# Prompt attention with undivided probabilities: low halves on GpSimd, weights' low halves on VectorE

## The chip, the cores and the metric

One NeuronCore of a Trainium2 chip runs the program. The metric is the time of one execution on the device in microseconds (us); of the kernel before, three runs are known. Times within a run are counted from the start of the profiled span.

## What is computed

The reference is one layer of a decoder step with 1024 prompt tokens and 8 sample tokens, model width 1024, all in float32. A normed input is projected (`w_in`); a third of the mixing width is attention, the rest a pooling mixer and a spatial-gating MLP; each is multiplied by a SiLU gate and all go through one output projection (`w_out`), a second norm and the residual. For the attention of the prompt (8 heads of 64, 2 key/value heads, an ALiBi slope per head) three branches are added, each with its own softmax and a sigmoid gate per token and head:

```python
s = jnp.where(mask, s, NEG_INF)
p = jnp.exp(s - jnp.max(s, axis=-1, keepdims=True)) * mask
return p / jnp.maximum(jnp.sum(p, axis=-1, keepdims=True), 1e-30)
...
o = gf[..., 0:1] * o_c + gf[..., 1:2] * o_s + gf[..., 2:3] * o_w
```

`o_c` attends to 16 compressed blocks, `o_s` to selected blocks (with 16 blocks in all these are all keys up to the token), `o_w` to a window of 512 keys.

## The kernel before

Float32 accuracy is kept on the matmul engine by splitting every operand into a high and a low float16 half; a product is then three matmuls (high by high, high by low, low by high). Weights are loaded in float32 by SyncE (`load_w`) or, for the output weights, by GpSimd (`load_wo`), ScalarE writes the high half (64 times the weight, line 254 or 1452) and the low half is made by VectorE in one operation (lines 260 and 1457) or by GpSimd in two (lines 257 and 258, 1454 and 1455). In the part that matters here, GpSimd makes them for six projection tiles (`if "attn" in hold`) and for every second output tile (`q % 2`).

The first 250 us project keys, values and queries and serve the sample tokens. Then `AT` is opened and the prompt's attention runs, from token tile 7 down to 0 (128 tokens each). Its work is cut into units (token tile, first head, number of heads): one head for tiles 7 to 3, two for tiles 2 and 1, four for tile 0, fifty units in all. Tile i has `i + 1` key tiles in the selected branch and `min(i + 1, 5)` in the window branch. The loop over `st` is a pipeline written out by hand. In step `st` it does:

* `norm_a` of the unit before: VectorE makes the factor gate / sum (lines 1328 and 1329), ScalarE writes the high half H of the divided probabilities, one copy per head and branch (line 1334);
* `qk` of the unit: scores on TensorE into the banks `s`; per branch VectorE adds slope and mask, keeps the row's minimum in `sm` (line 1320), and ScalarE takes the exponential and its sum (line 1322) into P, which has two buffers;
* `norm_b` of the unit before: VectorE writes the low half of the divided probabilities, one operation per head and branch (line 1343), and SyncE issues one transposing DMA from H (two buffers) to T (three buffers, line 1346);
* `take`: a budget of other work, that is the remaining projections (`tgroup`), pooling, gating and output projections (`outproj`); most chunks fill one of the two `fp` banks and are evicted by VectorE or ScalarE at the next `flush`;
* `pv` of the unit three steps back: per head and key tile one matmul of 128 columns (high T by high and low V) and one of 64 (low T by high V), both branches into the same columns; at the end of a half of the heads the compressed part is added with three matmuls of 256 columns;
* `combine` when half of the heads are done (line 1383 ff.): ScalarE and VectorE add the two column blocks, multiply by the gate, and write both halves for the output projection.

SyncE and GpSimd run in the written order; for the other engines the framework chooses an order that respects the dependencies. Waiting times for GpSimd are written down with `later(...)`, by which generators such as `post_u` and `gmlp` decide when their next part is emitted.

Of the kernel before, what the change touches and what calls it, by code (L numbers as in the profile page):

```python
# [20 lines left out]
EPS = 1e-6  # L21
SLOTS = [(k, g) for g in range(4) for k in range(2)]
# [28 lines left out]
def tile_hymba(ctx: ExitStack, tc: tile.TileContext, A: dict):  # L51
# [17 lines left out]
    # ------------------------------------------------------------ emission order  # L69
# [81 lines left out]
    # ------------------------------------------------------------ tiles  # L151
# [22 lines left out]
    rsc = C.tile([128, 8], F32, name="rsc")  # L174
    md = C.tile([128, 2, 4, 8], F16, name="md")
# [49 lines left out]
    # ------------------------------------------------------------ loads and splits  # L225
# [19 lines left out]
    def split_w(gi):  # L245
# [108 lines left out]
    # ------------------------------------------------------------ start: two column groups, contraction outermost  # L354
# [112 lines left out]
    def bcast():  # L467
        for q in range(2):
# [3 lines left out]
            def done(q=q, pr=pr):  # L472
                S.activation(R[:, q * 512:q * 512 + 512], pr, AF.Copy)
                if q == 1:
# [3 lines left out]
                    V.tensor_scalar(rsc, rst, 2.0 ** -17, None, ALU.mult)  # L478
                    V.tensor_scalar(psc2, ccd("psc"), 1.0 / 128, None, ALU.mult)
# [40 lines left out]
    # ------------------------------------------------------------ column groups, features on partitions  # L520
# [38 lines left out]
    # ------------------------------------------------------------ compressed keys and values  # L559
# [104 lines left out]
    # ------------------------------------------------------------ compressed attention of the prompt  # L664
# [47 lines left out]
    # ------------------------------------------------------------ decode attention  # L712
# [170 lines left out]
    # ------------------------------------------------------------ column groups, tokens on partitions  # L883
# [157 lines left out]
    # ------------------------------------------------------------ pooling and gating  # L1041
# [160 lines left out]
    # ------------------------------------------------------------ projections that attention needs, decode beside them  # L1202
# [51 lines left out]
    # ------------------------------------------------------------ prompt attention, the rest of the projections between  # L1254
# [4 lines left out]
    # kl and the high parts of q once more, on the other half of the partitions: two low passes run side by side  # L1259
# [16 lines left out]

    def qk(u):
# [3 lines left out]
        sm = AT.tile([128, nh, 4], F32, tag="sm", name=f"sm{i}_{s0}", bufs=4)  # L1281
        if s0 % 4 == 0 and (i, s0) != (0, 4):
            load_qx(*((i, 1) if s0 == 0 else (i - 1, 0)))
        for h in range(nh):
# [31 lines left out]
            for (br, n, o), (ps, z) in zip(spans(i), banks):  # L1316
# [4 lines left out]
                                       sm[:, h, br:br + 1])  # L1321
                S.activation(p, p, AF.Exp, bias=sm[:, h, br:br + 1], scale=-1.0, accum_out=sm[:, h, 2 + br:3 + br])  # L1322
        return P, sm

    def norm_a(u, P, sm):
        i, s0, nh = u
        nt = i + 1 + min(i + 1, 5)
        V.scalar_tensor_tensor(sm[:, :, 2:4], sm[:, :, 2:4], 1e-30, invg[:, i, s0:s0 + nh, 1:3], ALU.max, ALU.mult)  # L1328
        V.reciprocal(sm[:, :, 2:4], sm[:, :, 2:4])
        H = AT.tile([128, 2, nh, nt * 128], F16, tag="H", name=f"H{i}_{s0}", bufs=2)  # L1330
        for h in range(nh):
            for br, n, o in spans(i):
                c = slice(o * 128, (o + n) * 128)
                S.activation(H[:, 0, h, c], P[:, h, c], AF.Copy, scale=sm[:, h, 2 + br:3 + br])  # L1334
        return H

    def norm_b(u, P, sm, H):
        i, s0, nh = u
        nt = i + 1 + min(i + 1, 5)
        for h in range(nh):  # L1340
            for br, n, o in spans(i):
                c = slice(o * 128, (o + n) * 128)
# [6 lines left out]
    obank = {}  # L1349

    def pv(u, pt):
        i, s0, nh = u
        nt = i + 1 + min(i + 1, 5)
        if s0 % 4 == 0:
            obank[i, s0 // 4] = op.tile([128, 512], F32, tag="o", name=f"O{i}_{s0 // 4}")
        ob = obank[i, s0 // 4]
        for h in range(nh):
            s = s0 + h
            c = slice(s % 2 * 64, s % 2 * 64 + 64)
            o = ob[:, s % 4 * 128:s % 4 * 128 + 128]  # L1360
            first = s % 4 == 0
            for br, n, off in spans(i):
                for j in range(n):
# [5 lines left out]
        if (s0 + nh) % 4 == 0:  # L1369
            need(f"pct{i // 4}")  # L1370
            pct = hold[f"pct{i // 4}"]
            b0 = i % 4
            oh = ob.rearrange("p (s h d) -> p s h d", h=2, d=64)[:, :, 0]
# [443 lines left out]
```

## Time and profile before

| What | Value |
|---|---|
| Runs | 608.74 us median of 3 (608.67 to 609.25) |
| Profiled execution, span | 610.4 us |
| TensorE busy | 540.0 us (88%) |
| VectorE busy | 470.7 us (77%) |
| ScalarE busy | 340.2 us (56%) |
| GpSimd busy | 200.4 us (33%) |

The profiled execution is 1.7 us above the median. In the rows further down PE is TensorE (PEld its weight loads), DVE VectorE, ACT ScalarE, POOL GpSimd and SP SyncE; "L1343" is line 1343 of the kernel. A busy share is a mean over stages that are limited by different engines, so it is read by stage.

### The profile page before, as it was taken

What the parts mean: (1) busy time and instruction counts of PE and PEld (TensorE: products, weight loads), DVE (VectorE), ACT (ScalarE), POOL (GpSimd) and SP (SyncE); (2) the same over time, 40 slices, a digit from 0 to 9 for tenths busy, and PEclk for the clock granted to TensorE, in tenths of its full rate; (3) what the DMA queues carried; (4) which work ended last, traced back from release to release, by engine and by line L of the source; (5) the groups of instructions that cost most, each with busy time, mean ns of one, the idle gap of its engine ahead of it and who ended that gap; (6) DMA issues with size and microseconds to landing.
All of it is one profiled execution on the core that took longest, in us unless ns stands there. A gap on an engine that the chain in (4) does not pass through costs nothing.

```text
span 610.4 us, 13331 instructions
## 1 busy us (share of the span) xinstructions
PE 540.0 (88%) x5188; PEld 348.1 (57%) x5188; DVE 470.7 (77%) x900; ACT 340.2 (56%) x662; POOL 200.4 (33%) x149
## 2 busy tenths in 40 slices
PE   5899989889999997999888997884659999999995
PEld 2566645579768997456555654453225454455552
DVE  5975489995784673598899999976997678887743
ACT  6444344464543452468665665655567667786831
POOL 1884395202345000354534347224643200000001
PEclk9989999998999999899998999887577899999999
DMA  8614884454735626179796949669798779879683
GB/s 294 241 35 134 232 219 116 116 157 120 230 125 178 214 71 187 42 123 188 115 159 119 176 76 177 120 136 181 176 178 177 133 102 208 177 135 220 138 196 120
DMA packets 196882, 95.24 MB, mean 156 GB/s; under 512 B 166867, under 2 KB 185715, under 8 KB 196755
## 3 DMA queue, kind: packets, MB, share of 16 engines
q1 hardware_dynamic: 194018, 81.37, 61.0%
q0 software_dynamic: 2656, 12.77, 6.2%
q8 instruction: 40, 0.66, 0.4%
q10 hardware_dynamic: 144, 0.26, 0.1%
q14 instruction: 24, 0.19, 0.1%
HBM read 45.43 MB, written 11.86 MB: 94 GB/s over the span
## 4 chain that ended last, share of the span: by engine, by line
PE 47%; DMA 19%; DVE 17%; SPq 6%; issue 6%; ACT 4%; POOL 2%; DVEq 0%; POOLq 0%; ACTq 0%
PE op L67 12%; PE ps L67 11%; DMA T<-H 10%; PE s L67 7%; PE zps L67 5%; DVE H L1343 5%; PE O L67 5%; DVE P L1320 2%; PE v1ps L67 2%; SPq L310 2%; DMA xm<-in_xT_dram 1%; ACT P L1322 1%; DMA raw<-in_wt_dram 1%; DVE qa L518 1%; SPq L317 1%
## 5 line engine op out<-in xcount | busy, mean ns | idle before, releaser
L67 PE MATMUL ps<-xh,ws 128*128 128x344 f16 x768 | 178.7, 316 | 6.7 <-DVE t L490 3.9
L67 PEld LDWEIGHTS <-ws 128*128 128x128 f16 x1376 | 129.1, 100 | 91.4 <-issue 19.5
L1322 ACT ACTIVATE P<-P,sm 128x640 f32<-128x640 f32 (+7 forms) x128 | 92.7, 725 | 62.9 <-DVE sm L1320 52.0
L67 PE MATMUL ps<-xl,ws 128*128 128x344 f16 x384 | 121.3, 316 | 0.0
L1343 DVE SCALAR_TENSOR_TENSOR H<-P,sm,H 128x640 f16<-128x640 f32 (+7 forms) x128 | 109.9, 899 | 10.2 <-ACT H L1334 10.1
L67 PEld LDWEIGHTS <-qa 128*128 128x128 f16 (+1 forms) x612 | 47.9, 98 | 87.6 <-issue 59.2
L1334 ACT ACTIVATE H<-P,sm 128x640 f16<-128x640 f32 (+7 forms) x128 | 84.9, 722 | 16.1 <-DMA T<-H 13.3
L1320 DVE CUSTOM_DVE_ANT_0 P<-s,ctt 128x640 f32<-128x640 f32 (+7 forms) x128 | 85.6, 701 | 10.4 <-PE s L67 10.0
L67 PE MATMUL O<-vn,T 128*128 128x128 f16 (+1 forms) x1056 | 59.4, 216 | 18.5 <-DMA T<-H 18.4
L67 PE MATMUL s<-ka,qa 128*128 128x384 f16 (+4 forms) x192 | 54.0, 338 | 20.5 <-DVE sm L1320 20.5
L67 PEld LDWEIGHTS <-T 128*128 128x128 f16 x1056 | 53.5, 103 | 28.9 <-DMA T<-H 22.5
L67 PEld LDWEIGHTS <-xh 128*128 128x128 f16 x768 | 61.3, 99 | 0.7
L67 PE MATMUL op<-wo,qa 128*128 128x512 f16 x192 | 46.6, 387 | 0.5 <-DMA qa<-yza 0.5
L67 PE MATMUL zps<-ws,xh 128*128 128x128 f16 x512 | 45.0, 219 | 0.0
L67 PE MATMUL zps<-ws,xl 128*128 128x128 f16 x256 | 43.6, 219 | 0.0
L257 POOL TENSOR_SCALAR raw<-raw 128x1024 f32<-128x1024 f32 x6 | 18.0, 3008 | 73.8 <-ACT ws L254 73.8
L1490 POOL TENSOR_SCALAR sq<-sq 128x1 f32<-128x1 f32 x8 | 2.1, 266 | 115.5 <-ACT o L1520 115.5
L67 PEld LDWEIGHTS <-xl 128*128 128x128 f16 x384 | 38.0, 99 | 2.7 <-issue 2.1
L254 ACT ACTIVATE ws<-raw 128x1024 f16<-128x1024 f32 x21 | 22.2, 1057 | 21.8 <-PE ps L67 11.0
L67 PE MATMUL s<-kl,qa 64*128 64x384 f16 (+5 forms) x100 | 33.7, 344 | 0.0
L67 PE MATMUL s<-klx,qx 64*128 64x384 f16 (+4 forms) x92 | 30.6, 333 | 0.0
L1328 DVE SCALAR_TENSOR_TENSOR sm<-sm,invg 128x2 f32<-128x2 f32 (+2 forms) x50 | 21.1, 422 | 8.0 <-ACT P L1322 7.8
(329 smaller groups left out, 931.6 us busy)
## 6 DMA issues: line engine op xcount, KB each, us to landing
raw<-in_wt_dram SPq DMA_DIRECT2D x21, 512.0 KB, 4.2
wor<-in_wo_dram POOLq DMA_DIRECT2D x8, 512.0 KB, 5.5
xr<-in_xn_dram SPq DMA_DIRECT2D x8, 512.0 KB, 4.4
o_kww_dram<-in_cwin_dram POOLq DMA_DIRECT2D x1, 4088.0 KB, 17.0
o_y_dram<-o SPq DMA_DIRECT2D x7, 512.0 KB, 4.2
cr<-in_ccmp_dram SPq DMA_DIRECT2D x24, 128.0 KB, 2.8
xq<-in_xT_dram SPq DMA_DIRECT2D x3, 516.0 KB, 8.5
kr<-in_cselk_dram SPq DMA_DIRECT2D x20, 64.0 KB, 2.0
```

The lines of the kernel that those rows point to most:

```text
L67: nc.tensor.matmul(out, lhsT=l, rhs=r, start=st, stop=en)
L254: S.activation(ws[:, 0, :, a:b], r, AF.Copy, scale=64.0)
L257: G.tensor_scalar(r, r, 64.0, None, ALU.mult)
L310: Y.dma_start(t[:, :, j * 128:(j + 1) * 128], A["ccmp"][page(b, j)].rearrange("o p (r c) -> (o p) r c", r=2))
L317: Y.dma_start(t[:, 0, j * 128:(j + 1) * 128], A["csel" + kv][page(b, j)].rearrange("o p c -> (o p) c"))
L518: V.tensor_tensor(qa[b:b + 64, :, 2 * g + k], tv[a:a + 64], qa[a:a + 64, :, 2 * g + k], ALU.subtract)
L1320: V.tensor_tensor_reduce(p, ps[:, z:z + T], ctt[:, end - T:end], -slope, 3e38, ALU.add, ALU.min, sm[:, h, br:br + 1])
L1322: S.activation(p, p, AF.Exp, bias=sm[:, h, br:br + 1], scale=-1.0, accum_out=sm[:, h, 2 + br:3 + br])
L1328: V.scalar_tensor_tensor(sm[:, :, 2:4], sm[:, :, 2:4], 1e-30, invg[:, i, s0:s0 + nh, 1:3], ALU.max, ALU.mult)
L1334: S.activation(H[:, 0, h, c], P[:, h, c], AF.Copy, scale=sm[:, h, 2 + br:3 + br])
L1343: V.scalar_tensor_tensor(H[:, 1, h, c], P[:, h, c], sm[:, h, 2 + br:3 + br], H[:, 0, h, c], ALU.mult, ALU.subtract)
L1490: G.tensor_scalar(sq[:, 2:3], sq[:, 1:2], 1.0 / 1024, sq[:, 0:1], ALU.mult, ALU.add)
```

## The change

In `qk`, both score passes of a head come first, then one addition of LN = ln 1024 to the head's two minima, then both exponentials. Right after, ScalarE writes the high half of the undivided probabilities, one copy for the whole unit. `norm_a` goes. `norm_b` becomes `low`: GpSimd subtracts H from P in one operation for the unit, then the transposing DMA is issued as before. `pv` keeps the branches apart, with three matmuls of 64 columns per key tile, and the compressed part moves to a bank and a tile of its own (`cmp_out`, once per token tile, ahead of the first unit's PV). `combine` divides: it makes the factors for four heads and two branches, multiplies, and adds the two branches and the compressed part. All weights' low halves go to VectorE. The sums of a token tile live in one tile (`sums`), and the memory for software DMA descriptors is set to 8192.

```diff
             S.activation(ws[:, 0, :, a:b], r, AF.Copy, scale=64.0)
-            if "attn" in hold:
-                later(3.8)
-                G.tensor_scalar(r, r, 64.0, None, ALU.mult)
-                G.tensor_tensor(ws[:, 1, :, a:b], r, ws[:, 0, :, a:b], ALU.subtract)
-            else:
+            if True:
                 V.scalar_tensor_tensor(ws[:, 1, :, a:b], r, 64.0, ws[:, 0, :, a:b], ALU.mult, ALU.subtract)
...
                 V.tensor_tensor_reduce(p, ps[:, z:z + T], ctt[:, end - T:end], -slope, 3e38, ALU.add, ALU.min,
-                                       sm[:, h, br:br + 1])
-                S.activation(p, p, AF.Exp, bias=sm[:, h, br:br + 1], scale=-1.0, accum_out=sm[:, h, 2 + br:3 + br])
+                                       sm[:, s, br:br + 1])
+            V.tensor_scalar(sm[:, s, 0:2], sm[:, s, 0:2], LN, None, ALU.add)
+            for br, n, o in spans(i):
+                p = P[:, h, o * 128:o * 128 + n * 128]
+                S.activation(p, p, AF.Exp, bias=sm[:, s, br:br + 1], scale=-1.0, accum_out=sm[:, s, 2 + br:3 + br])
+        H = AT.tile([128, 2, nh, nt * 128], F16, tag="H", name=f"H{i}_{s0}", bufs=2)
+        S.activation(H[:, 0], P, AF.Copy)
...
-                V.scalar_tensor_tensor(H[:, 1, h, c], P[:, h, c], sm[:, h, 2 + br:3 + br], H[:, 0, h, c],
-                                       ALU.mult, ALU.subtract)
+        G.tensor_tensor(H[:, 1], P, H[:, 0], ALU.subtract)
...
+    def cmp_out(i):
+        need(f"pct{i // 4}")
+        pct = hold[f"pct{i // 4}"]
+        b0 = i % 4
+        ps = fp.tile([128, 512], F32, tag="f", name=f"oc{i}")
+        for h in range(2):
+            c = slice(h * 256, h * 256 + 256)
+            mm(ps[:, c], pct[:, b0], vbd[:, 0, c], h == 0, False)
+            mm(ps[:, c], pct[:, b0], vbd[:, 1, c], False, False)
+            mm(ps[:, c], pct[:, b0 + 4], vbd[:, 0, c], False, h == 1)
+        oc = ocs[i] = AT.tile([128, 512], F32, tag="oc", name=f"ocs{i}", bufs=1)
+        S.activation(oc, ps, AF.Copy, scale=rsc[:, i:i + 1])
...
-                    mm(o, pt[:, q], vn[br][:, kt:kt + 10:9, c], first, False)
+                    mm(o, pt[:, q], vn[br][:, kt, c], first, False)
                     first = False
-                    mm(o[:, 0:64], pt[:, nh * nt + q], vn[br][:, kt, c], False, False)
+                    mm(o, pt[:, q], vn[br][:, kt + 9, c], False, False)
+                    mm(o, pt[:, nh * nt + q], vn[br][:, kt, c], False, last)
...
+        V.scalar_tensor_tensor(sc, sums[i][:, h * 4:h * 4 + 4, 2:4], 1e-30, invg[:, i, h * 4:h * 4 + 4, 1:3],
+                               ALU.max, ALU.mult)
+        V.reciprocal(sc, sc)
+        V.tensor_scalar(sc, sc, rsc2[:, i:i + 1], None, ALU.mult)
+        t2 = AT.tile([128, 4, 2, 64], F32, tag="mt", name=f"mt{i}_{h}", bufs=1)
+        V.tensor_tensor(t2, ob, sc.unsqueeze(3).to_broadcast([128, 4, 2, 64]), ALU.mult)
+        t = t2[:, :, 0]
+        V.tensor_tensor(t, t, t2[:, :, 1], ALU.add)
+        V.tensor_tensor(t, t, ocs[i][:, c].rearrange("p (s d) -> p s d", d=64), ALU.add)
...
-            if q % 2:
-                G.tensor_scalar(raw, raw, 64.0, None, ALU.mult)
-                G.tensor_tensor(w[:, 1], raw, w[:, 0], ALU.subtract)
-            else:
-                V.scalar_tensor_tensor(w[:, 1], raw, 64.0, w[:, 0], ALU.mult, ALU.subtract)
+            V.scalar_tensor_tensor(w[:, 1], raw, 64.0, w[:, 0], ALU.mult, ALU.subtract)
...
-    nc = bacc.Bacc("TRN2", target_bir_lowering=False, num_devices=1)
+    nc = bacc.Bacc("TRN2", target_bir_lowering=False, num_devices=1, dynamic_dma_scratch_size=8192)
```

## Rows read from the trace of the kernel before

**Rows 1.** The chain that ended last, by line, share of the span.

```profile
PE op L67 12%; PE ps L67 11%; DMA T<-H 10%; PE s L67 7%; PE zps L67 5%; DVE H L1343 5%; PE O L67 5%; DVE P L1320 2%; PE v1ps L67 2%; SPq L310 2%; DMA xm<-in_xT_dram 1%; ACT P L1322 1%; DMA raw<-in_wt_dram 1%; DVE qa L518 1%; SPq L317 1%
```

**Rows 2.** Busy time by stretch: us, busy (instructions), granted clock, DMA share, GB/s.

```profile
250.00:311.00 61.00, 57.73 (x546) 35.45 (x543) 52.13 (x95) 40.36 (x66) 26.63 (x11) 1.00 0.70 125
311.00:370.00 59.00, 52.60 (x550) 33.45 (x547) 57.18 (x99) 36.57 (x60) 26.95 (x19) 0.94 0.74 139
370.00:436.00 66.00, 43.70 (x383) 26.92 (x383) 55.68 (x109) 37.28 (x65) 28.91 (x24) 0.83 0.79 156
436.00:484.00 48.00, 40.01 (x389) 21.86 (x387) 39.15 (x78) 31.13 (x60) 17.76 (x10) 0.73 0.85 159
484.00:590.00 106.00, 105.43 (x758) 53.47 (x755) 80.79 (x263) 74.74 (x221) 4.87 (x12) 1.00 0.86 168
```

**Rows 3.** Groups by line (busy, mean ns, idle before), then line 1343 alone by stretch.

```profile
L1343 DVE SCALAR_TENSOR_TENSOR H<-P,sm,H 128x640 f16<-128x640 f32 (+7 forms) x128 | 109.9, 899 | 10.2 <-ACT H L1334 10.1
...
L1328 DVE SCALAR_TENSOR_TENSOR sm<-sm,invg 128x2 f32<-128x2 f32 (+2 forms) x50 | 21.1, 422 | 8.0 <-ACT P L1322 7.8
...
L1334 ACT ACTIVATE H<-P,sm 128x640 f16<-128x640 f32 x28 | 21.9, 815 | 5.1 <-DMA T<-H 5.1
...
L1334 ACT ACTIVATE H<-P,sm 128x128 f16<-128x128 f32 x16 | 4.9, 387 | 0.0
...
250.00:484.00 234.00, 79.43 (x66) 0.88 0.77 144
484.00:590.00 106.00, 30.42 (x62) 1.00 0.86 168
```

**Rows 4.** Timeline (start, us), VectorE beside GpSimd; one group; one line's min/median/max.

```profile
276.73 2.17 DVE L1328 SCALAR_TENSOR_TENSOR sm<-sm,invg 128x2 f32<-128x2 f32 x1 [0.29 <-ACT P L1322]
...
276.52 2.37 POOL L1080 TENSOR_TENSOR yc<-yc,t 128x1032 f32<-128x1032 f32 x1 [5.66 <-DVE yc L1103]
...
348.23 1.70 DVE L1156 COPY dsh<-t 128x8 f32<-128x8 f32 x1
...
347.77 2.12 POOL L258 TENSOR_TENSOR ws<-raw,ws 128x1024 f16<-128x1024 f32 x1
...
176.13 0.20 DVE L819 TENSOR_SCALAR sm<-sm,igd 128x1 f32<-128x1 f32 x1
...
172.39 4.52 POOL L980 TENSOR_TENSOR vbig<-vbig,gnb 128x2048 f32<-128x2048 f32 x1 [5.91 <-DVE vbig L979]
...
L1329 DVE RECIPROCAL sm<-sm 128x2 f32<-128x2 f32 x40 | 6.4, 160 | 0.6
```

**Rows 5.** Groups by line and shape: prices of VectorE and GpSimd operations.

```profile
L1521 DVE TENSOR_TENSOR o<-op,gpb 128x512 f32<-128x512 f32 x16 | 11.0, 689 | 14.6 <-ACT o L1520 14.5
...
L1457 DVE SCALAR_TENSOR_TENSOR wo<-wor,wo 128x1024 f16<-128x1024 f32 x4 | 4.8, 1212 | 0.0
...
L257 POOL TENSOR_SCALAR raw<-raw 128x1024 f32<-128x1024 f32 x6 | 18.0, 3008 | 73.8 <-ACT ws L254 73.8
...
L258 POOL TENSOR_TENSOR ws<-raw,ws 128x1024 f16<-128x1024 f32 x6 | 12.9, 2157 | 0.5
```

**Rows 6.** Waits from 250 to 484 us (total, times, longest); T's issues there, us to landing.

```profile
ACT H L1334 <- DMA T<-H: 9.9, 6, 5.1
...
DVE dsh L1156 <- DMA o_ps_dram<-dsh: 4.8, 1, 4.8
...
T<-H SPq DMA_TRANSPOSE x32, 5.8
```

**Rows 7.** TensorE's timeline: a run of PV matmuls, a run of narrow ones, and what follows each.

```profile
483.03 1.01 PE L67 MATMUL O<-vn,T 128*128 128x128 f16 x20
483.88 0.38 PE L67 MATMUL op<-wo,qa 128*128 128x512 f16 x1
...
468.52 0.34 PE L67 MATMUL dops<-md,wo 128*128 128x16 f16 x8
468.73 0.24 PE L67 MATMUL dops<-mxp,wo 128*128 128x16 f16 x4
```

More of the change, by code (lines that the diff above doesn't have):

```diff
@@ L21 @@
 EPS = 1e-6
+LN = 10 * float(np.log(2.0))
 SLOTS = [(k, g) for g in range(4) for k in range(2)]
@@ L174, in tile_hymba @@
     rsc = C.tile([128, 8], F32, name="rsc")
+    rsc2 = C.tile([128, 8], F32, name="rsc2")
     md = C.tile([128, 2, 4, 8], F16, name="md")
@@ L1275, in spans @@
         return (0, i + 1, 0), (1, n, i + 1)
+    sums = {}
     def qk(u):
@@ L1280, in qk @@
         P = AT.tile([128, nh, nt * 128], F32, tag="P", name=f"P{i}_{s0}", bufs=2)
-        sm = AT.tile([128, nh, 4], F32, tag="sm", name=f"sm{i}_{s0}", bufs=4)
+        if s0 == 0:
+            sums[i] = AT.tile([128, 8, 4], F32, tag="sm", name=f"sm{i}", bufs=2)
+        sm = sums[i]
         if s0 % 4 == 0 and (i, s0) != (0, 4):
@@ L1320, in qk, with low @@
                 V.tensor_tensor_reduce(p, ps[:, z:z + T], ctt[:, end - T:end], -slope, 3e38, ALU.add, ALU.min,
-                                       sm[:, h, br:br + 1])
-                S.activation(p, p, AF.Exp, bias=sm[:, h, br:br + 1], scale=-1.0, accum_out=sm[:, h, 2 + br:3 + br])
-        return P, sm
-    def norm_a(u, P, sm):
+                                       sm[:, s, br:br + 1])
[5 more added lines that the diff above has]
+        S.activation(H[:, 0], P, AF.Copy)
+        return P, H
+    def low(u, P, H):
         i, s0, nh = u
         nt = i + 1 + min(i + 1, 5)
[L1328 to L1342, printed above, removed]
-                V.scalar_tensor_tensor(H[:, 1, h, c], P[:, h, c], sm[:, h, 2 + br:3 + br], H[:, 0, h, c],
-                                       ALU.mult, ALU.subtract)
+        G.tensor_tensor(H[:, 1], P, H[:, 0], ALU.subtract)
         pt = AT.tile([128, 2 * nh * nt, 128], F16, tag="T", name=f"T{i}_{s0}", bufs=3)
@@ L1349, in tile_hymba @@
     obank = {}
+    ocs = {}
+    def cmp_out(i):
[10 more added lines that the diff above has]
+        S.activation(oc, ps, AF.Copy, scale=rsc[:, i:i + 1])
     def pv(u, pt):
@@ L1353, in pv @@
         nt = i + 1 + min(i + 1, 5)
+        if s0 == 0:
+            cmp_out(i)
         if s0 % 4 == 0:
@@ L1365, in pv @@
                     q = h * nt + off + j
-                    mm(o, pt[:, q], vn[br][:, kt:kt + 10:9, c], first, False)
+                    last = s % 4 == 3 and br == 1 and j == n - 1
+                    mm(o, pt[:, q], vn[br][:, kt, c], first, False)
                     first = False
-                    mm(o[:, 0:64], pt[:, nh * nt + q], vn[br][:, kt, c], False, False)
[L1369 to L1373, printed above, removed]
-            c = slice(s0 // 4 * 256, s0 // 4 * 256 + 256)
-            mm(oh, pct[:, b0], vbd[:, 0, c], False, False)
-            mm(oh, pct[:, b0], vbd[:, 1, c], False, False)
-            mm(oh, pct[:, b0 + 4], vbd[:, 0, c], False, True)
+                    mm(o, pt[:, q], vn[br][:, kt + 9, c], False, False)
@@ L1379, in combine @@
+                    mm(o, pt[:, nh * nt + q], vn[br][:, kt, c], False, last)
     def combine(i, h):
-        ob = obank.pop((i, h)).rearrange("p (s h d) -> p s h d", h=2, d=64)
+        ob = obank.pop((i, h)).rearrange("p (s r d) -> p s r d", r=2, d=64)
         c = slice(h * 256, h * 256 + 256)
-        t = AT.tile([128, 4, 64], F32, tag="mt", name=f"mt{i}_{h}", bufs=1)
-        S.activation(t, ob[:, :, 1], AF.Copy, scale=rsc[:, i:i + 1])
-        V.scalar_tensor_tensor(t, ob[:, :, 0], rsc[:, i:i + 1], t, ALU.mult, ALU.add)
@@ L1385, in combine @@
-        tf = t.rearrange("p s d -> p (s d)")
+        sc = AT.tile([128, 4, 2], F32, tag="asc", name=f"as{i}_{h}", bufs=2)
+        V.scalar_tensor_tensor(sc, sums[i][:, h * 4:h * 4 + 4, 2:4], 1e-30, invg[:, i, h * 4:h * 4 + 4, 1:3],
[4 more added lines that the diff above has]
+        V.tensor_tensor(t2, ob, sc.unsqueeze(3).to_broadcast([128, 4, 2, 64]), ALU.mult)
@@ L1391, in combine @@
         yield
-        V.tensor_tensor(hl[:, a + 256:a + 512], tf, hl[:, a:a + 256], ALU.subtract)
+        V.tensor_tensor(hl[:, a + 256:a + 512].rearrange("p (s d) -> p s d", d=64), tf,
+                        hl[:, a:a + 256].rearrange("p (s d) -> p s d", d=64), ALU.subtract)
         if h == 1:
@@ L1626, in tile_hymba @@
         if u is not None:
-            pend[u] = norm_b(u, P, sm, H)
+            pend[u] = low(u, *pend[u])
         bg_step()
```

11 lines of the change are left out of this document (5 added, 6 removed).

## The prediction

> **What bounds the kernel now.** I read the chain of waits first [rows 1]: behind TensorE's matmuls stand the transposes of the probabilities (DMA T<-H, 10%) and VectorE's pass for their low halves (DVE H, 5%). Then the busy table, cut where the first transpose of token tiles 7, 6, 5, 4 and 3 is issued [rows 2]. From 250 to 484 us VectorE is busy 52.1 + 57.2 + 55.7 + 39.2 = 204 of 234 us, and TensorE only 194, partly at a granted clock of 0.83 and 0.73. From 484 to 590 us TensorE is busy 105.4 of 106 us. So there is room before 484 and hardly any behind it.
>
> Third, the groups [rows 3]: line 1343, the VectorE pass that goes away, is 109.9 us, of which 79.4 us lie before 484. Last, what holds VectorE itself. An operation of line 1328 on two elements took 2.17 us from 276.73 and ended 0.01 us behind a GpSimd TENSOR_TENSOR that began at 276.52 and took 2.37; a COPY of eight elements took 1.70 us and ended with the GpSimd operation of 347.77 [rows 4]. So VectorE operations with two SBUF inputs, and at least some with one, stand still while GpSimd works on two tensors. RECIPROCAL never did (mean 160 ns over 40 [rows 4]).
>
> **The change, part by part.** Times are against the profiled execution (610.4 us, 1.7 above the median 608.74); the difference is then taken from the median.
>
> *VectorE, removed before 484 us.* Line 1343: 79.4 us [rows 3]. The scale and reciprocal per unit (lines 1328 and 1329): 21.1 us for 50 of the first [rows 3] and 50 x 0.16 = 8 for the second; 32 of 50 units have their low halves before 484, and line 1328's long waits lie mostly there, so I take 23 us.
>
> *VectorE, added before 484 us.* Low halves of nine of the ten weight tiles that GpSimd has now: 9 x 1.21 = 10.9 (row of line 1457 [rows 5]). The LN addition on two elements, one per head and there one per unit: 32 x 0.16 = 5.1. Combine, per half tile: three operations on eight elements (3 x 0.16), a 512-wide product out of PSUM (0.69, row of line 1521) [rows 5] and two 256-wide additions (half of that and something for the start: 0.42 each); the one 256-wide operation of line 1384 goes (0.42 as well): 2.0 - 0.4 = 1.6, seven halves, 11.2. Together 27.2.
>
> *GpSimd.* One subtraction per unit. Line 258 does the same with the same types: 2157 ns for 1024 elements, 2.11 ns each [rows 5]. A head has 128 x (13, 12, 11, 10, 8, 6, 4, 2) elements for tiles 7 to 0, so eight heads of all tiles have 67584: 142 us, 99 before 484. What leaves: ten splits at 3.01 + 2.16 [rows 5], 52 us, nine of them (46.5) before 484. GpSimd now has 26.6 + 27.0 + 28.9 + 17.8 = 100 us there [rows 2]; then 99 + 54 = 153 of 234, 65%. It isn't full, but it holds VectorE as seen [rows 4].
>
> *What that lock costs VectorE.* The LN addition stands between both score passes and both exponentials of a head. Its bounds: nothing (the one-element TENSOR_SCALAR of line 819 took 0.20 us within a GpSimd TENSOR_TENSOR [rows 4]) and one whole subtraction each time (3.50 us for tile 7: 99 us over the stage). I take a wait, since the COPY on an even number waited: 65% hits x half an operation (1.55) = 1.0 us, 32 us in all. The Trainium skill, "VectorE: DVE Perf Modes", section "Mode 2×_2P — use both read ports for one tensor", has a TENSOR_SCALAR from SBUF use both read ports where the outermost dimension is even, and its "GPSIMD Engine Reference", "Key points", names contention with such instructions: by it the addition waits, as taken here. By the one-element row alone the sum would be 32 us lower. Two waits in each of seven combines (14 us) and one in each of nine splits (9 us) come on top: 55 us.
>
> VectorE's sum before 484: -79.4 - 23 + 27.2 + 55 = -20.2 us.
>
> *The way of a unit to its matmuls.* A copy of 128 elements takes 387 ns, one of 640 takes 815 [rows 3]: 0.28 us plus 0.84 ns per element. ScalarE makes 50 copies for 128, which saves 78 x 0.28 = 22 us, and the eight copies of 512 for the compressed part (0.7 each) about balance the sixteen that leave combine; ScalarE is busy 62% before 484 [rows 2], so this is off the path. The subtraction takes longer than what it replaces (3.50 against 1.2 us per thousand elements on VectorE, 2.0 for the unit), and stands behind GpSimd's other operations: 54 / 32 = 1.7 us per unit, of which half the units meet one. That makes T about 0.8 us later beyond what the waits of line 1343 cost now. Behind the transpose on SyncE wait the qx loads, later the residual loads and output stores; TensorE waits for T at the end of the third step after the scores, so I let a third reach it: 32 x 0.8 / 3 = +8.5 us. H has two buffers: the copy of a unit now comes a step earlier and waits, with ScalarE's exponentials and evictions behind it, until T of the unit but one before has landed (5.8 us; that wait is 9.9 us today [rows 6]). The loop copy + subtraction + landing, shared by two units, is (1.67 + 3.50 + 5.8) / 2 = 5.5 us for tile 7, 5.3, 5.1 and 4.9 for the next, against steps of 7.6, 7.4, 8.3 and 6.0 now, the stretches over eight units [rows 2]: no bound yet.
>
> *TensorE.* Two PV matmuls (128 and 64 columns) become three of 64. Twenty took 483.88 - 483.03 = 0.85 us, 42.5 ns each, and eight with 8 and 16 columns, a new weight tile each, took 0.21 us, 26 ns [rows 7]. Three at 29 ns (26.7 for 64 columns at 2.4 GHz plus the 2.5 by which 42.5 exceeds the mean of 96) are 87 against 85 ns: 528 times, +1.3 us. The compressed part keeps its 48 matmuls but takes one of the two bank buffers that the projections use, once per tile: bounds nothing and, were each of eight to wait for one VectorE hold, 8 x 1.55; inside the 8.5 above.
>
> *Edits at nothing.* From 484 us TensorE covers VectorE's 30.4 us less [rows 3]; if that cover goes, it is gain. The last combine, which nothing covers, is longer by one addition and the wider product, less the ScalarE copy ahead of it: +0.6. The smaller DMA scratch touches GpSimd's own transfers; if one had to wait for another to land, the nearest row is a landing of 5.8 us [rows 6]; I take nothing. The dropped waiting time in the written order lets consumers be queued earlier, some ScalarE operations then ahead of a later GpSimd result; also taken into the 8.5. The store that makes VectorE wait 4.8 us [rows 6] stays.
>
> **Sum:** -20.2 + 8.5 + 1.3 + 0.6 = -9.8 us: 600.6 for the profiled execution, 599 for the median.
>
> **Rivals.**
> *The relief comes through whole* (chance 0.15): the additions slip between the subtractions, and TensorE's own work is the floor before 484: 194 us at the clocks granted now [rows 2], so up to -40, that is 569. For it: the steps of tiles 5 and 4 are long where TensorE idles. Against: every lock row.
> *Each addition meets the subtraction of the unit ahead* (0.24, the other side): then a unit's step is addition, two exponentials, copy, subtraction in a row: 0.16 + 1.14 + 0.82 + 1.67 + 3.50 = 7.3 us for tile 7, 6.8, 6.3 and 5.9 for the next, over eight units each 210 us, and GpSimd's other 54 us stand partly in that row. It is slower than the 234 us of now once more than 24 of the 54 lie there; at two thirds, 246: +12, so 621; at all, 264 and 639. For it: in-order engines and the holds seen [rows 4]; against: TensorE may run one unit ahead, and then the addition comes before the subtraction starts.
> *Nothing that can be measured* (0.08): the stage ends by T's transposes beside the weight loads, whoever makes the low halves: 609.
> *The extra weight loads count* (0.02): 528 more at the 42.5 ns of a PV matmul, +22: 631. Against it: 26 ns each with few columns [rows 7]. The Trainium skill, "TensorE: Matmul & The Clock Gate", section "Back-to-back issue gap", gives about 81 ns per pair with 128 columns; by it, it would be +43. The trace has half of that for 128 and 64 mixed.
>
> **How the numbers follow.** My own case has 0.51: -9.8 with the lock between 40 and 65 us, so 584 to 609; some 0.04 of it ends above no change. About 0.2% (1.2 us) is what a measurement of this kernel can tell from none. Faster: 0.15 + 0.47 = 0.62; same: 0.08 + 0.01 = 0.09; slower: 0.24 + 0.02 + 0.03 = 0.29. The range, 578 to 618, takes in the milder ends of the first two rivals.
>
> **What would show it.** Right: line 1343 gone, GpSimd 65% busy before 484 with subtractions near 3.5, 3.2, 3.0 and 2.7 us, VectorE's LN additions often far over 0.16 us and ending with a GpSimd operation, tile 5's stretch the one that shrinks most, the stretch from 484 on unchanged, PV matmuls 29 ns apart. Wrong: additions that never wait (then the first rival), or steps of 7 us with exponentials waiting for the addition and TensorE for T (the second).

## The result, and the profile after

The changed kernel takes **647.0 us** (median of 4 runs, 642.8 to 648.3) against 608.7 for the kernel before (604.9 to 609.3): ratio 1.062, 95% interval 1.058 to 1.067. The forecast was 599.0 us with a range up to 618; the result is slower, and outside it. The profiled execution has a span of 646.1 us, 35.7 more than that of before. Medians, here and below, are of all executions of a kernel, while ratios and intervals leave out single executions over 1.5% longer than the fastest of the same kernel, so that a ratio can differ a little from that of the medians.

The page of after: busy time by engine, the chain by engine and by line (it answers to [rows 1]), and three groups.

```profile
PE 551.8 (85%) x5716; PEld 353.2 (55%) x5716; DVE 465.4 (72%) x827; ACT 321.2 (50%) x576; POOL 290.5 (45%) x179
...
PE 33%; DVE 27%; DMA 16%; issue 8%; ACT 7%; SPq 7%; POOL 3%; DVEq 0%; POOLq 0%; ACTq 0%
PE ps L68 8%; PE op L68 8%; DMA T<-H 7%; DVE P L1323 5%; PE zps L68 5%; PE s L68 3%; ACT P L1328 3%; POOL H L1336 2%; SPq L308 2%; DVE sm L1325 2%; PE v1ps L68 2%; ACT H L1330 2%; PE O L68 1%; DVE mt L1391 1%; DMA xm<-in_xT_dram 1%
...
L1336 POOL TENSOR_TENSOR H<-P,H 128x1024 f16<-128x1024 f32 (+4 forms) x50 | 140.7, 2816 | 210.7 <-ACT H L1330 195.3
...
L1328 ACT ACTIVATE P<-P,sm 128x640 f32<-128x640 f32 (+7 forms) x128 | 92.7, 725 | 105.8 <-DVE sm L1325 105.7
...
L1325 DVE TENSOR_SCALAR sm<-sm 128x2 f32<-128x2 f32 x64 | 41.6, 657 | 0.5
```

VectorE is only 5 us less busy than before although a pass of 109.9 us [rows 3] is gone; GpSimd has 90 us more. The subtraction costs what line 258 promised, 2.1 ns per element: 140.7 us, forecast 142. The chain is no longer one of matmuls and transposes: VectorE's score passes, its LN addition, ScalarE's exponentials and GpSimd's subtraction stand in it.

The busy time by stretch answers to [rows 2]: cuts at the first transpose of tiles 6, 5, 4 and 3; columns TensorE, its weight loads, VectorE, ScalarE, GpSimd, granted clock, DMA share, GB/s.

```profile
250.00:317.00 67.00, 61.66 (x695) 38.47 (x693) 47.43 (x81) 41.46 (x59) 43.30 (x15) 1.00 0.66 128
317.00:373.00 56.00, 46.60 (x596) 29.67 (x595) 48.80 (x79) 30.77 (x47) 33.48 (x12) 0.91 0.74 136
373.00:428.00 55.00, 42.56 (x448) 26.59 (x445) 46.38 (x85) 28.77 (x46) 39.78 (x27) 0.91 0.77 130
428.00:496.00 68.00, 39.16 (x314) 17.84 (x311) 50.43 (x78) 34.22 (x55) 34.25 (x23) 0.60 0.78 156
...
496.00:646.00 150.00, 134.95 (x1174) 69.65 (x1172) 93.40 (x260) 70.06 (x188) 49.29 (x35) 0.94 0.64 136
```

The last stretch of before, to its end, in the same view:

```profile
484.00:610.00 126.00, 118.84 (x828) 59.60 (x824) 88.77 (x277) 78.80 (x232) 6.48 (x16) 0.99 0.79 164
```

Before had 61, 59, 66, 48 and 126 us; its cut at 311 lies 3 us ahead of the first transpose of tile 6 (313.94), so tiles 7 and 6 are taken together here. Tiles 7 and 6 together are 3 us longer, tile 5 is 11 us shorter, tile 4 is 20 us longer and the rest 24 us longer. Up to the cut ahead of tile 3, VectorE is busy 193 us where before had 204, and yet the stage takes 246 us and not 234. TensorE is busy 190 us of it, so neither engine fills the stage. In tile 4's stretch TensorE has 39 us of work in 68 and a granted clock of 0.60, which is mostly the lower of its two levels (1.2 and 2.4 GHz); it idles 29 us there. What is late there is the output projection. Its matmuls with attention inputs, first in before, then in after (ns min/median/max, first and last start in us):

```profile
L67 PE MATMUL op<-wo,qa x192: 376/379/634, 451.8 to 603.6; 128*128 128x512 f16 x192
```
```profile
L68 PE MATMUL op<-wo,qa x192: 376/379/634, 493.8 to 639.2; 128*128 128x512 f16 x192
```

From the first of them to the end of the span it is 159 us before and 152 after. So the loss is made ahead of them, and much of it shows itself as work pushed back into the last stretch.

How one unit loses, from the timeline of after (start, us, engine, line; in brackets the idle time ahead and what ended it):

```profile
404.43 3.34 SPq L1338 DMA_TRANSPOSE T<-H  x1
...
406.07 0.82 DVE L1323 CUSTOM_DVE_ANT_0 P<-s,ctt 128x640 f32<-128x640 f32 x1
406.43 2.85 POOL L1336 TENSOR_TENSOR H<-P,H 128x1408 f16<-128x1408 f32 x1 [3.67 <-ACT H L1330]
...
407.42 1.89 DVE L1325 TENSOR_SCALAR sm<-sm 128x2 f32<-128x2 f32 x1
...
409.41 0.93 ACT L1328 ACTIVATE P<-P,sm 128x768 f32<-128x768 f32 x1 [3.10 <-DVE sm L1325]
...
412.96 1.94 PE L68 MATMUL O<-vn,T 128*128 128x64 f16 x33 [5.02 <-DMA T<-H]
413.00 1.38 ACT L1330 ACTIVATE H<-P 128x1408 f16<-128x1408 f32 x1 [1.16 <-DMA T<-H]
...
414.71 0.72 PE L68 MATMUL s<-ka,qa 128*128 128x384 f16 x2
```

The LN addition on two elements began at 407.42 and ended at 409.31, 0.03 us behind the subtraction of the unit ahead (406.43 + 2.85); ScalarE's exponentials stood 3.1 us for it. TensorE stood 5.0 us for another thing: the T of an earlier unit, by the order of the units the one issued at 404.43, which landed some 8.5 us later; ScalarE's next copy waited for a T at the same time.

### The profile page after: what moved, and what is told of

Read it like the earlier page. It is cut to its first block, busy times and chain, and to the rows that moved or that the text cites. A ratio compares the mean times of both kernels' runs of the same rounds, so it can differ in the third digit from the quotient of the medians.

```text
span 646.1 us, 14254 instructions
## 1 busy us (share of the span) xinstructions
PE 551.8 (85%) x5716; PEld 353.2 (55%) x5716; DVE 465.4 (72%) x827; ACT 321.2 (50%) x576; POOL 290.5 (45%) x179
## 4 chain that ended last, share of the span: by engine, by line
PE 33%; DVE 27%; DMA 16%; issue 8%; ACT 7%; SPq 7%; POOL 3%; DVEq 0%; POOLq 0%; ACTq 0%
PE ps L68 8%; PE op L68 8%; DMA T<-H 7%; DVE P L1323 5%; PE zps L68 5%; PE s L68 3%; ACT P L1328 3%; POOL H L1336 2%; SPq L308 2%; DVE sm L1325 2%; PE v1ps L68 2%; ACT H L1330 2%; PE O L68 1%; DVE mt L1391 1%; DMA xm<-in_xT_dram 1%
## 5 line engine op out<-in xcount | busy, mean ns | idle before, releaser
L1336 POOL TENSOR_TENSOR H<-P,H 128x1024 f16<-128x1024 f32 (+4 forms) x50 | 140.7, 2816 | 210.7 <-ACT H L1330 195.3
L68 PE MATMUL s<-ka,qa 128*128 128x384 f16 (+4 forms) x192 | 56.5, 352 | 31.2 <-DVE sm L1323 31.1
L68 PE MATMUL O<-vn,T 128*128 128x64 f16 x1584 | 61.1, 201 | 16.7 <-DMA T<-H 16.7
L1330 ACT ACTIVATE H<-P 128x1024 f16<-128x1024 f32 (+4 forms) x50 | 66.3, 1325 | 14.7 <-DMA T<-H 13.8
L68 PEld LDWEIGHTS <-T 128*128 128x128 f16 x1584 | 57.7, 103 | 26.7 <-DMA T<-H 19.4
L1325 DVE TENSOR_SCALAR sm<-sm 128x2 f32<-128x2 f32 x64 | 41.6, 657 | 0.5
L258 DVE SCALAR_TENSOR_TENSOR ws<-raw,ws 128x1024 f16<-128x1024 f32 x21 | 30.8, 1469 | 10.1 <-ACT ws L256 10.1
L68 PE MATMUL s<-klx,qx 64*128 64x384 f16 (+4 forms) x92 | 32.0, 348 | 0.0
L68 PE MATMUL op<-wo,mxg 128*128 128x512 f16 x96 | 26.6, 410 | 2.9 <-ACT wo L1461 1.5
```

What stands on the lines that cost most here:

```text
L68: nc.tensor.matmul(out, lhsT=l, rhs=r, start=st, stop=en)
L1325: V.tensor_scalar(sm[:, s, 0:2], sm[:, s, 0:2], LN, None, ALU.add)
L1330: S.activation(H[:, 0], P, AF.Copy)
L1336: G.tensor_tensor(H[:, 1], P, H[:, 0], ALU.subtract)
```

## The experiments

Differences are of medians; the kernel before had 608.6 to 609.1 us beside them. Several kernels, the base among them (599.4 and 604.6), have two executions only, with intervals of up to 1.7% to either side: a difference of a few us between two such kernels is not told apart from none. "Base" is the changed kernel with both of the first two edits below undone: no LN addition, and the low half made by VectorE, one operation per unit.

### Which part costs: addition or subtraction

**No LN addition**, each exponential behind its own score pass. This leaves out the factor 1024 of the probabilities.

```diff
-            V.tensor_scalar(sm[:, s, 0:2], sm[:, s, 0:2], LN, None, ALU.add)
-            for br, n, o in spans(i):
-                p = P[:, h, o * 128:o * 128 + n * 128]
```

> The changed kernel without the LN addition (probabilities then lie up to 1 instead of 1024, the factor cancels in the division) and with each exponential again right behind its own score pass. Theory 1, the addition: it stands before both exponentials of a head, took 41.6 us of VectorE with its holds, and ScalarE waited 105.7 us for it; without it 25 us or more of the 38 come back: 610 to 622. Theory 2, the subtraction on GpSimd: its holds and its length stay, so 638 to 647. Theory 3, combine on VectorE, which now waits in order for PV matmuls and exponentials: 640 to 647.

Measured: 629.0 us (ratio 1.034, 1.017 to 1.050): 18 us less than after, between the first two theories. Its two executions took 625.7 and 632.3.

**The addition on one element, twice.**

```diff
-            V.tensor_scalar(sm[:, s, 0:2], sm[:, s, 0:2], LN, None, ALU.add)
+            for br in range(2):
+                V.tensor_scalar(sm[:, s, br:br + 1], sm[:, s, br:br + 1], LN, None, ALU.add)
```

> The changed kernel with the LN addition written as two additions on one element each; order and place stay. If the hold by GpSimd is what the addition costs (theory 1a), one-element additions pass within GpSimd's operation, the group takes some 128 x 0.16 = 20 us in place of 41.6 and the time falls by 10 to 25 us. If its place in VectorE's queue and the wait for both passes cost (theory 1b), the time stays within 5 us. Theories 2 and 3: within 5 us.

Measured: 632.0 us (1.039, 1.027 to 1.051). The order of the operations is that of after, so 15 of the 18 us are the hold; the 3 that would be left for the order lie within the spread. The line of the addition in after, then the same in this kernel (ns min/median/max):

```profile
L1325 DVE TENSOR_SCALAR sm<-sm x64: 116/163/4571, 253.7 to 604.7; 128x2 f32<-128x2 f32 x64
```
```profile
L1326 DVE TENSOR_SCALAR sm<-sm x128: 96/144/155, 249.1 to 588.9; 128x1 f32<-128x1 f32 x128
```

On two elements it takes up to 4.6 us, on one never more than 0.155. The Trainium skill, "VectorE: DVE Perf Modes", section "Mode 2×_2P — use both read ports for one tensor", names an even outermost dimension as a condition for a TENSOR_SCALAR to use both read ports; two elements meet it and one does not. The two rows agree, though they show the hold and not the ports.

**The low half by VectorE**, one operation per unit, the addition kept; and then **both edits**, the base.

```diff
-        G.tensor_tensor(H[:, 1], P, H[:, 0], ALU.subtract)
+        V.tensor_tensor(H[:, 1], P, H[:, 0], ALU.subtract)
```

> The changed kernel with the low half subtracted by VectorE, still one operation per unit (1.8 us for tile 7 against 3.4); all else as changed. Theory 2: no holds from it and a path shorter by 1.6 us per unit: 25 us or more come back, 610 to 622. Theory 1: VectorE has about 75 us more work, the addition then is not held but stands behind it: 640 to 650. Theory 3: 640 to 655.

> Both of the above: no addition, exponential behind its own pass, low halves by VectorE in one operation per unit. What is left of the change is the undivided copy by unit, the three PV matmuls, the compressed part's own bank, combine's division and the weights. Theories 1 and 2 together: 600 to 612, at or a little under the kernel before. Theory 3 (combine) or the weights: 625 or more stays.

Measured: 605.8 us (0.994, 0.990 to 0.999) and 602.0 (0.989, 0.975 to 1.003). The move of the subtraction alone costs 41 us. The addition costs 18 us beside it and 4, within the spread, without it. The rest of the change (undivided probabilities, one copy and one low half per unit, the division in combine, the weights) gains some 7 us; the interval of the base takes in no change, but a kernel one edit away (601.5, below) is clear of it.

### What the subtraction costs with: holds, GpSimd's queue, or T coming late

**A useless subtraction beside VectorE's own**, of the same size and types, into a tile that nobody reads: on the low-half kernel of 605.8 us, and on the base.

```diff
         V.tensor_tensor(H[:, 1], P, H[:, 0], ALU.subtract)
+        N = nh * nt * 128
+        G.tensor_tensor(dmy[:, 0:N], ctt[:, 0:N], H[:, 1].rearrange("p h c -> p (h c)"), ALU.subtract)
```

> The kernel with the low halves by VectorE (605.8 us), and beside it on GpSimd, for each unit, a subtraction of the same size and types into a tile that nobody reads, begun when the low half is written. It is an extra, no output depends on it. It gives VectorE the same holds (140 us of GpSimd on two tensors) without standing between a unit's copy and its transposing DMA. If the holds are what the subtraction on GpSimd cost: 630 to 650, most of the 41 us again. If its length and its place behind GpSimd's other work cost: 603 to 615.

> The kernel without the addition and with the low halves by VectorE (602.0 us), and per unit a subtraction of two tensors on GpSimd into a tile that nobody reads, begun when the low half is written: an extra without use. It holds VectorE's operations with two SBUF inputs, but no score pass and no addition. If what counts is the hold of any VectorE operation in its queue: 625 to 640. If the holds of the addition carried nearly all of the earlier 46 us: 603 to 615.

Measured: 652.5 us (1.064, 1.056 to 1.073) and 649.3 (1.066, 1.062 to 1.071): +47 us each time. T waits for nothing new, so GpSimd's work makes the loss by itself.

**The same on half the elements**, on the kernel of 605.8 us.

```diff
+        N = nh * nt * 64
+        G.tensor_tensor(dmy[:, 0:N], ctt[:, 0:N], H[:, 1].rearrange("p h c -> p (h c)")[:, 0:N], ALU.subtract)
```

> The kernel with the low halves by VectorE and the addition (605.8 us) with the useless subtraction of two tensors at half its length per unit (70 us in all in place of 140; at the full length it was 652.5 us). If the loss follows the time that GpSimd holds: half of 47 us, 622 to 635. If only holds as long as a step matter: 606 to 615.

Measured: 628.8 us (1.033, 1.028 to 1.037), +23: the cost goes about with the length. The waiting for each unit, priced below, is in both.

**One-tensor work in its place**, on the base.

```diff
+        hb = H[:, 1].rearrange("p h c -> p (h c)").bitcast(F32)
+        G.tensor_scalar(dmy[:, 0:N // 2], hb, 64.0, None, ALU.mult)
+        G.tensor_scalar(dmy[:, 0:N // 4], hb[:, 0:N // 4], 64.0, None, ALU.mult)
```

> The same, but GpSimd works on one tensor per operation, two operations per unit of together about the same length, into a tile that nobody reads: an extra without use. If the shared way to SBUF is the cause, VectorE's operations with two inputs pass and the time stays near 602, at most 612. If GpSimd being busy at all (its queue, later work behind it) is the cause: as with two tensors, 625 to 640.

Measured: 627.2 us (1.030, 1.026 to 1.035), +25, between the two. The groups show that it hardly holds VectorE: VectorE's own low half takes 1633 ns here, close to the 1599 of the base, and 1891 beside two-tensor work. In turn: base, useless subtraction, one-tensor work:

```profile
L1333 DVE TENSOR_TENSOR H<-P,H 128x1024 f16<-128x1024 f32 (+4 forms) x50 | 79.9, 1599 | 12.3 <-ACT H L1327 12.1
```
```profile
L1335 POOL TENSOR_TENSOR dmy<-ctt,H 128x1024 f16<-128x1024 f32 (+4 forms) x50 | 146.9, 2938 | 182.9 <-DVE H L1333 169.3 <-DVE as L1384 7.7 <-DVE do L1560 2.1
L1333 DVE TENSOR_TENSOR H<-P,H 128x1024 f16<-128x1024 f32 (+4 forms) x50 | 94.6, 1891 | 10.1 <-ACT H L1327 9.9
```
```profile
L1336 POOL TENSOR_SCALAR dmy<-H 128x512 f32<-128x512 f32 (+4 forms) x50 | 100.8, 2016 | 156.0 <-DVE H L1333 154.2 <-DVE as L1386 0.9
L1333 DVE TENSOR_TENSOR H<-P,H 128x1024 f16<-128x1024 f32 (+4 forms) x50 | 81.6, 1633 | 16.7 <-ACT H L1327 16.6
L1337 POOL TENSOR_SCALAR dmy<-H 128x256 f32<-128x256 f32 (+4 forms) x50 | 66.4, 1328 | 4.1
```

VectorE's busy time in all is 460 us in the base, 471 beside the one-tensor work and 532 beside the two-tensor work. So there is a second cost beside the holds. The next two try to take it apart.

**Waiting without work**, on the base: one element of each unit's low half.

```diff
+        G.tensor_scalar(dmy[:, 0:1], H[:, 1].rearrange("p h c -> p (h c)").bitcast(F32)[:, 0:1], 64.0, None, ALU.mult)
```

> The kernel after, without the LN addition, low halves by VectorE (602 us), plus per unit a GpSimd operation on one element of the low half: it makes GpSimd's queue wait for each unit's low half but takes next to no time and holds nothing. Theory Q (the cost comes because the pooling and gating operations and the loads of the output weights stand in GpSimd's queue behind operations that wait for their unit; the last pooling operation ran at 436 us without these, at 470 us in the one-tensor and half-size experiments, both 25 us dearer): 620 to 630 us, the last pooling operation at 460 us or later. Theory H (VectorE held by two-tensor work costs the time): 600 to 605 us. Output unchanged.

Measured: 611.0 us (1.002, 0.998 to 1.006), +9, between the two: GpSimd's queue, made to wait for each unit, costs a little by itself. The operations took 0.28 us each, 14 in all, and the last pooling operation began at 451 us. All ten executions (606.2 to 617.9) are above the two of the base.

**Work without waiting**, on the base: two-tensor work on constant tiles.

```diff
+        N = nh * nt * 64
+        for _ in range(2):
+            G.tensor_tensor(dmy[:, 0:N], dmc[:, 0:N], dmy[:, 0:N], ALU.subtract)
```

> The same kernel of 602 us plus useless two-tensor GpSimd work of the same elements and types per unit, in two halves, on constant tiles, so that it waits for nothing. GpSimd is as busy as in the kernel after (some 140 us more), but its other work never stands behind an operation that waits. H: 640 to 652 us, VectorE's operations lengthened by some 70 us. Q: 602 to 615 us, the last pooling operation before 450 us. Output unchanged.

Measured: 643.6 us (1.058, 1.053 to 1.063), +42. The holds' expectation is met; but this work took 188 us, not 147, and it also keeps GpSimd from its own work: the last pooling operation began at 482.5 us, where 450 or less was expected and the base has 436.1. So this run does not part the holds from GpSimd's late work. It reads no H, and so excludes one more rival as the main cause of the losses above, that GpSimd's reading gives H's buffers back later. GpSimd's last load of output weights and last pooling operation, in before, then in after, from the timeline:

```profile
438.82 1.14 POOL L1427 DMA_DIRECT2D wor<-in_wo_dram  x2 [0.30 <-POOL wo L1455]
443.60 2.14 POOL L1183 TENSOR_TENSOR mxp<-yzb,mxp 128x1032 f16<-128x1032 f32 x1 [3.65 <-ACT mxp L1182]
```
```profile
474.43 2.60 POOL L1336 TENSOR_TENSOR H<-P,H 128x1280 f16<-128x1280 f32 x1 [10.87 <-ACT H L1330]
476.98 1.09 POOL L1436 DMA_DIRECT2D wor<-in_wo_dram  x2
478.08 2.62 POOL L1336 TENSOR_TENSOR H<-P,H 128x1280 f16<-128x1280 f32 x1
480.64 0.56 POOL L1436 DMA_DIRECT2D wor<-in_wo_dram  x1
481.22 2.15 POOL L1182 TENSOR_TENSOR mxp<-yzb,mxp 128x1032 f16<-128x1032 f32 x1
```

In after the loads stand in order behind subtractions, one of which had GpSimd wait 10.9 us for ScalarE's copy, and the output projections need both. This is the likely second cost. How the 47 us divide is bounded, not settled: 9 us are waiting alone; 25 come with one-tensor work that holds VectorE hardly at all, though it kept GpSimd busy longer (167 us); so some 22 at least come only with two-tensor work.

**The subtraction on GpSimd for a part of the tiles**, on the base: tiles 3 to 0 (`i <= 3`), and tiles 7 to 5 (`i >= 5`).

```diff
-        V.tensor_tensor(H[:, 1], P, H[:, 0], ALU.subtract)
+        (G if i <= 3 else V).tensor_tensor(H[:, 1], P, H[:, 0], ALU.subtract)
```

> The same kernel of 602 us with the subtraction on GpSimd for tiles 3 to 0 only (some 43 of 142 us of it), where GpSimd's pooling and gating work is nearly done. H: the cost goes with the two-tensor time, 43/142 of 47 us, so 613 to 617 us. Q: 598 to 605 us. Output unchanged.

> The same kernel of 602 us with the subtraction on GpSimd for tiles 7 to 5 only (some 78 of 142 us of it), where GpSimd has its pooling and gating work. H: 78/142 of 47 us, so 624 to 630 us, most of it lost in the stretches of tiles 7 to 5 themselves. Q: 615 to 630 us, most of it lost behind them, in tiles 4 and 3, where the output projections come late. Output unchanged.

Measured: 605.5 us (0.994, 0.990 to 0.997) and 611.9 (1.004, 1.000 to 1.008). These expectations forgot that VectorE is relieved in turn: against the 27 us of the kernel without the addition, shares of 43/142 and 78/142 are 8 and 15. Measured are 3.5 and 10. The first lies at the edge of the expectation from GpSimd's queue and is not told apart from the base, the second lies below both. The two parts make half of the 27 us; tile 4, which is the rest of the units, was not tried alone, and what the parts have in common stays open.

### What the relief of VectorE is worth

**No low half at all**, on the base: two fixed tiles hold H, and the transposes take what stands in their second half.

```diff
-        V.tensor_tensor(H[:, 1], P, H[:, 0], ALU.subtract)
+        Hn[0] += 1
+        H = Hf[Hn[0] % 2][:, 0:2 * nh * nt * 128].rearrange("p (a h c) -> p a h c", a=2, h=nh)
```

(The second line takes the place of H's allocation in `qk`.)

> The kernel of 602 us (VectorE's low halves, no LN addition) with no low half of the probabilities made by any engine: two fixed tiles hold H, and the transposing DMA takes whatever stands in their second half. It takes 80 us off VectorE, holds nothing and lets T start earlier. If VectorE's time were path one for one, as the forecast's sum has it: 530 to 555 us. If the relief is what the runs so far make it (649 with useless subtractions beside VectorE's own, 629 with GpSimd's alone, so 20 us for the same 80): 578 to 588 us. The low halves are left out of the output.

Measured: 582.0 us (0.951, 0.943 to 0.958): 20 us for 80 us of VectorE. Its busy times:

```profile
PE 526.7 (91%) x5716; PEld 343.6 (59%) x5716; DVE 383.5 (66%) x765; ACT 322.3 (56%) x576; POOL 147.5 (25%) x129
...
300.00:350.00 50.00, 50.00 (x688) 32.96 (x687) 36.45 (x80) 36.93 (x55) 14.16 (x11) 1.00 1.08 194
350.00:400.00 50.00, 41.16 (x451) 25.89 (x449) 31.47 (x80) 28.51 (x47) 12.27 (x15) 0.93 0.85 131
400.00:450.00 50.00, 37.98 (x509) 22.15 (x508) 31.23 (x68) 35.93 (x60) 9.21 (x11) 0.90 0.98 209
```

VectorE falls to 66%, but TensorE reaches 91% and is full from 300 to 350 us: there is nothing left to gain there. From 350 to 450 us it is busy 79 of 100 us and VectorE 63, so neither is the bound; what is was not tried.

**The same, with GpSimd subtracting into a tile that nobody reads.**

```diff
+        N = nh * nt * 128
+        G.tensor_tensor(dmy[:, 0:N], P.rearrange("p h c -> p (h c)"), H[:, 0].rearrange("p h c -> p (h c)"), ALU.subtract)
```

> The same, with GpSimd subtracting H from P into a tile that nobody reads: the holds and the waiting in GpSimd's queue are those of the kernel with the low halves on GpSimd and no LN addition (629 us), but T does not wait for the subtraction. If the holds make the loss: 620 to 632 us, some 40 to 47 us above the kernel without any low half. If T's lateness makes it: 585 to 600 us. The low halves are left out of the output.

Measured: 621.0 us (1.022, 1.018 to 1.026), +39. VectorE does the same work in both, and its busy time rises from 383.5 to 453.8 us, so the holds are 70 us of VectorE:

```profile
PE 535.5 (87%) x5716; PEld 346.9 (56%) x5716; DVE 453.8 (74%) x765; ACT 323.0 (52%) x576; POOL 291.2 (47%) x179
```

The kernel that uses this subtraction and has no addition takes 629.0: T's lateness is the remaining 8 us, as far as two executions of that kernel (625.7 and 632.3) tell.

### The other parts, and a better kernel

**The weights' low halves alone**: on the kernel before, all by VectorE; on the base, back to GpSimd (the branches of `load_w` and `split_wo` as before).

> The kernel before with one part of the change alone: VectorE makes all low halves of the weights, GpSimd none. If that part helps by itself: 600 to 606. If it only loads VectorE, which is busy 204 of 234 us before 484: 610 to 620.

> The kernel without the addition and with the low halves by VectorE (602.0 us), and the low halves of the weights given back to GpSimd as before the change (ten tiles, two operations each). If VectorE's making them is worth something (shorter way to the weights, fewer holds): 605 to 615. If the ten operations on VectorE are a burden of 12 us: 594 to 600.

Measured: 611.3 us (1.006, 1.002 to 1.010), so +3 us for that edit alone; and 607.3 us (0.988, 0.980 to 0.996), which is not told apart from the base.

**ScalarE takes O out of PSUM** in combine, on the base; the same kernel was measured a second time with more runs.

```diff
-        V.tensor_tensor(t2, ob, sc.unsqueeze(3).to_broadcast([128, 4, 2, 64]), ALU.mult)
+        S.activation(t2, ob, AF.Copy)
+        V.tensor_tensor(t2, t2, sc.unsqueeze(3).to_broadcast([128, 4, 2, 64]), ALU.mult)
```

> The kernel without the addition and with the low halves by VectorE (602.0 us), combine's first operation split: ScalarE copies the 512 columns out of PSUM and VectorE multiplies from SBUF, so that ScalarE and not VectorE is the one that waits in order for the PV matmuls. Theory 3, that this wait on VectorE costs: 594 to 599. Otherwise the added 0.7 us per half: 601 to 606.

> The best version so far again (no addition, low halves by VectorE in one operation per unit, PSUM read by ScalarE in combine, weights by VectorE), for its interval against the kernel before: 597 to 604, faster by 1 to 2%.

Measured: 600.6 us (0.980, 0.972 to 0.987), then 601.5 (0.989, 0.985 to 0.993). The edit itself isn't told apart from the base, but the kernel beats the one before by 1.1%: the change without its move to GpSimd and without the addition.

## Why the prediction was wrong

The runs lead from before to after by four steps that add up: 608.7 to 582.0 with all of the change but a low half and the addition (-27); GpSimd's work, 621.0 (+39); T waiting for it, 629.0 (+8); the addition, 647.0 (+18). Both last steps go by the two executions of the kernel of 629.0, so only their sum, 26, is firm.

* **"VectorE's sum ... -20.2 us": the step that failed.** It took 79.4 + 23 us off VectorE, put 27.2 on, and counted the -75.2 that are left as path, one for one, against the lock. The relief is worth 27 us, and the 80 us of the low half in it 20. Busy time of VectorE was not path: up to the cut it fell from 204 to 193 us (forecast: 184), and the stage grew by 12. The forecast's own floor, TensorE's 194 of 234 us [rows 2], capped the first rival at -40; it had to cap the relief in the sum as well, before the lock was added. -40 with its other terms is +25, the right sign, though even that cap is above the 27 measured.
* **"What that lock costs VectorE": 55 us up to the cut, about the right size, its parts off both ways.** The additions: 32 forecast for the stage; there the rows of line 1325 give 29.2 less 33 x 0.163, that is 24 (31 over the whole kernel); of path they cost 15. The combines' operations: 14 us forecast for seven half tiles; five of their lines (1387 to 1400) are longer there by 18 us than at their medians, and by 27 over all sixteen combines. The weights' low halves: 9 forecast, 7 found. That is 49 of the 55. Line 1325 by stretch, then one of the five lines:

```profile
250.00:496.00 246.00, 29.18 (x33) 0.85 0.73 138
496.00:646.00 150.00, 12.47 (x31) 0.94 0.64 136
...
L1391 DVE TENSOR_TENSOR mt<-mt x16: 412/425/2597, 292.7 to 626.7; 128x256 f32<-128x256 f32 x16
...
L1391 DVE TENSOR_TENSOR mt<-mt 128x256 f32<-128x256 f32 x16 | 14.1, 880 | 0.3
```

* **"It isn't full, but it holds VectorE": half the story of GpSimd's queue.** The forecast let the subtraction stand behind GpSimd's other operations (54 / 32 = 1.7 us per unit), but not the other way round: pooling, gating and the weight loads behind subtractions that wait. The one-tensor work puts this at up to 25 us.
* **T later, +8.5 us: not contradicted.** The 8 us above are counted from a kernel whose T waits for no low half at all, and the forecast's from one whose T waits for VectorE's, so the agreement of the two numbers is luck.
* **"From 484 us TensorE covers": failed, the second step to do so.** By the forecast's own numbers 142 - 99 = 43 us of subtractions lie there, and it gave them no cost. GpSimd is busy 49 us there, not 6, and the stretch is 24 us longer. TensorE is busy 16 us more (118.8 to 135.0); by the granted clocks of 0.99 and 0.94 some 9 of them are an estimate of work that came late, the others the lower clock. The subtractions of these tiles alone, on GpSimd, cost 3.5 us (605.5 against 602.0), not told apart from nothing, so most of the loss came from ahead.
* **TensorE's matmuls: right at the higher clock.** Thirty-three PV matmuls of 64 columns began at 405.59, and the next score matmul at 406.56:

```profile
405.59 1.14 PE L68 MATMUL O<-vn,T 128*128 128x64 f16 x33
406.56 0.49 PE L68 MATMUL s<-ka,qa 128*128 128x384 f16 x2
```

That is 0.97 / 33 = 29 ns each, as forecast. At the lower clock, behind TensorE's wait of 5.0 us above, they took (414.71 - 412.96) / 33 = 53 ns (granted clock 0.50), which the forecast did not price. The Trainium skill, "TensorE: Matmul & The Clock Gate", section "Back-to-back issue gap", gives about 81 ns for a matmul of 128 columns with its weight load; the PV matmuls of after have 64 columns and can't test that figure. What the forecast worked out from it for one rival, +43 us for 528 more matmuls, did not come.
* **The stages:** subtractions were to take 3.5, 3.2, 3.0 and 2.7 us; tiles 7, 5 and 4 have 3.37, 2.92 and 2.61. GpSimd is busy 151 of 246 us up to the cut, 61%, where 65% was forecast. Tile 5's stretch shrank most, as said; tile 4's growth was not foreseen.
* **The rivals.** The second, *each addition meets the subtraction of the unit ahead*, named the sign and, at "all", 639 us. Its mechanism is there (407.42 above) but is 15 to 18 of 38 us: without any addition the kernel is still 20 us slower than before. The first, 569 us, was not reached even by the kernel without any low half (582).

## What to carry to other kernels

Relief of a busy engine is worth at most what the next engine's floor leaves: cap it first, then add the new costs, which have no such cap. Here 80 us off VectorE were worth 20, and 70 us of holds came with 39. Work on two tensors on GpSimd costs three ways beside its own time: some of VectorE's operations stand until it ends (not the score passes, whose longest is 1.225 us with and without it), GpSimd's own later work (weight loads too) stands behind it and behind what it waits for, and its consumer may get its data later. Try such a move with the work on GpSimd left unused, and with the work left out: the two together price it.

## What the runs showed that was not expected

An operation of VectorE on two tensors holds GpSimd's one-tensor work as well, if it begins first. In the one-tensor experiment VectorE's low half ran from 300.14 for 1.83 us, and the GpSimd operation on 416 elements that began just behind it took 2.85 us, against 1.25 for the same form five microseconds later, which began 0.10 us ahead of VectorE's next low half. That low half took 2.04 us, against 1.75 for most of its shape in the base, and so did not wait for GpSimd's operation to end:

```profile
300.14 1.83 DVE L1333 TENSOR_TENSOR H<-P,H 128x1664 f16<-128x1664 f32 x1
300.23 2.85 POOL L1337 TENSOR_SCALAR dmy<-H 128x416 f32<-128x416 f32 x1
...
305.54 1.25 POOL L1337 TENSOR_SCALAR dmy<-H 128x416 f32<-128x416 f32 x1
305.64 2.04 DVE L1333 TENSOR_TENSOR H<-P,H 128x1536 f16<-128x1536 f32 x1 [1.02 <-ACT H L1327]
```
